# Operand tiles of 512-column matmuls moved to addresses congruent modulo 512 bytes, in a two-sequence encoder layer

## The chip, the cores and the metric

The kernel is one program on one core of a Trainium2 chip. The metric is the device time of one execution in microseconds (us); of several executions the median counts. The core's engines each work through a queue of their own: TensorE (PE in the profile; its weight loads are PEld), VectorE (DVE), ScalarE (ACT), GpSimd (POOL) and SyncE (SP, which here only starts transfers). They meet through semaphores. The on-chip memory, SBUF, has 128 partitions; "address" below is a byte offset within a partition, the same for all 128.

## The reference

One layer of an encoder, applied to two sequences (prompt and sample) of 1024 rows by 1024 columns, all in float32:

```python
h = rmsnorm(x, g_mix) * (1 + sc1) + sh1
q_lat, kv_lat, k_pe, f_in = split(h @ w_in)      # 256, 128, 64, 512 columns
y_mla  = mla_group(q_lat, kv_lat, k_pe, ...)     # 4 heads of latent attention with a rotary part
y_four = fourier_group(f_in, w_four)             # Re(FFT over rows and group columns), then 8 small products
x  = x + ga1 * (concat([y_mla, y_four]) @ w_out)
h2 = rmsnorm(x, g_ffn) * (1 + sc2) + sh2
y  = x + ga2 * ((silu(h2 @ w_gate) * (h2 @ w_up)) @ w_down)    # inner width 2816
return rmsnorm(y, g_final)
```

The six vectors sc1 to ga2 come from a small product of each sequence's conditioning vector.

## The kernel before

**Precision.** Every large float32 operand is kept as two tiles: a rounded high part (ScalarE's CAST, line 62, in `split`) and the remainder (VectorE's subtraction, line 63). A product is then three matmuls, high by high, high by low and low by high, lines 78, 79 and 80 in `mm3`. In `mm3(out, lh, ll, rh, rl, ...)` the l operands are stationary (128 columns, loaded as weights) and the r operands are moving (here mostly 512 columns, in the Fourier and attention parts also 448, 280, 258 or 256).

**Stages**, in the order of TensorE's queue and with their place in the profiled execution. Weights are folded and modulation vectors made (0 to 60 us); the input projection follows (to about 235). The Fourier part (238 to 330) multiplies by cosine and sine tables (`dft`): A holds the even-symmetric half of the frequencies, in 514 columns per 128 rows (512, and one pair of columns, 512 and 513, for frequency 512 and its filler), B the odd half in 512, `nyt` a few rows of Nyquist terms. `fourier_out` multiplies A, B and nyt, as stationary 128-column pieces, by folded weights `wm` and `wn`; the column pair goes through a product of its own for j = 0 (lines 774 to 779). Attention (332 to 769) runs 64 items (sequence s, query block b of 256 rows, head h, half u): `absorb_q` and `rope_q` make the query pieces qa and qp, `scores` multiplies them (stationary) by the latents `lat` (moving, 512 columns, 5 x 2 matmuls per item, lines 924 to 928), a softmax follows, `flip_p` transposes, `values` multiplies ckv by the probabilities, `out_proj` multiplies the result o by wv and adds it to x2. `norm2` squares (ScalarE, line 874), makes the reciprocal root (POOL, `rstd`) and scales (VectorE, line 879); the transposed result goes out to DRAM.

**The FFN** uses a seven-product scheme of the Strassen kind on 2 x 2 blocks. For each sequence the seven combinations of the input, H[0] to H[6], stand in SBUF as pairs of tiles, high H00, H10 ... H60 and low H01 ... H61, 4 x 512 columns each; `prep_h` fills them in the order HK = (0, 5, 1, 6, 4, 3, 2) by way of staging tiles H20, H21, H30, H31, X0. In the up projection (sequence 0: 778.8 to 1217.9; sequence 1: 1429.9 to 1870.1) each of 22 blocks of gate and up weights is combined into seven tiles (`sums_w`, lines 135 and 138), split into wh and wl (`hl`), and multiplied: 22 x 7 x 4 x 3 = 1848 matmuls per sequence, stationary wh or wl, moving H. In the down projection (1217.9 to 1429.9 and 1870 to 2051.5) both operands are tiles of the wh and wl rings. The last product of sequence 1 (2051.5 to 2081.6) uses H tiles on both sides, which by then hold other operands (`prep_last`).

**Memory.** Tiles are taken from pools that follow each other in the same addresses. A pool lays its tags out in the order in which the code first asks for them. Several small tiles named "phase..." hold nothing: they shift what is laid out behind them by 32 bytes. p3e is the pool of attention that `stage3_loads` lays out; p5, the pool of the FFN with all H tiles, starts at the same address when p3e is closed. A tile of p5 can be written only when the last reader of the p3e tile that it overlaps is done; the framework adds a wait for this, unless it follows from an earlier one.

**Order.** Each engine runs its queue in the order the code emits, apart from `issue_after` and `first`, which pin pieces of the transition to places behind named instructions. At the transition from attention to the FFN (lines 1014 to 1021 and 1154 to 1193) the last items of attention, `out_proj(1,2,...)`, the first H tiles (H00 and H01 from staging H20), the combinations w0 (written into H41) and `norm2` are interleaved so. `gbank` has two PSUM banks shared by `values` and `out_proj`.

Of the kernel before, what the change touches and what calls it, by code (L numbers as in the profile page):

```python
# [21 lines left out]
P = 128  # L22
# [30 lines left out]
def hybrid_encoder_kernel(ctx: ExitStack, tc: tile.TileContext, a: dict):  # L53
# [4 lines left out]
    def rd(t):  # L58
        return t.bitcast(F32)
# [104 lines left out]
    with ExitStack() as st:  # L164
# [13 lines left out]

        w.tile([P, 8], F32, name="phase_hh")
        wuqT = w.tile([P, HEADS, QL], F32, tag="hh0", name="wuqT")  # L180
        wq = w.tile([P, 2, 768], F32, tag="hl0", name="wq")
        w.tile([P, 8], F32, name="phase_wz")
        wz_h = w.tile([P, NC, DZ], F32R, name="wz_h")
# [404 lines left out]
    def load_q(s, b):  # L588
# [3 lines left out]
        S["q", s, b] = ql  # L592

    def rope_q(s, b, u, bankf):
        ql = S["q", s, b]
# [12 lines left out]
        here["p"] = nc.gpsimd.tensor_tensor(out=t1[:, 0], in0=t1[:, 0], in1=t1[:, 1], op=ALU.add).ins  # L608
        sk = e.tile([P, HEADS, P], F32R, tag="sk", name="qsk", bufs=2)
        nc.scalar.copy(sk[:, :, :64], t1[:, 0])  # L610
# [3 lines left out]
    def rope_flip(s, b, u, pt):  # L614
        sk = S.pop(("sk", s, b, u))
        for h in range(HEADS):
            nc.tensor.transpose(pt[:, h, :], sk[:, h, :], identr)
        qp = e.tile([P, HEADS, P], F32R, tag="qp", name="qp", bufs=4)
        nc.scalar.copy(qp, rd(pt))
        S["qp", s, b, u] = qp  # L620

    def absorb_q(s, b, h, bankf):
        ql = S["q", s, b]
        pq = bankf()
        hs = slice(h * P, h * P + P)
        for c in range(2):
            mm3(pq[:, :256], wq_h[:, c, hs], wq_l[:, c, hs], ql[0][:, c, :], ql[1][:, c, :], c == 0, c == 1)
        qa = [e.tile([P, 256], F32R, tag=f"qa{i}", name=f"qa{i}", bufs=3) for i in range(2)]
# [25 lines left out]
    with ExitStack() as st:  # L654
# [36 lines left out]
        def dft(s):  # L691
            z, od = zh.pop(s)
            A = [w.tile([P, 2, 528], F32R, tag=f"A{i}", name=f"A{i}", bufs=1)[:, :, :NT] for i in range(2)]
            B = [w.tile([P, 2, 512], F32R, tag=f"B{i}", name=f"B{i}", bufs=1) for i in range(2)]
            for q in (0, 2, 1) if s == 0 else (0, 1):
# [12 lines left out]
                if q == 2:  # L708
                    ah = w.tile([NY2, 528], F32R, name="nyh")[:, :NT]
                    al = w.tile([NY2, 528], F32, name="nyl")[:, :NT]  # L710
                else:
                    ah, al = A[0][:, q, :], A[1][:, q, :]
                for o, v in ((slice(0, 256), pe[:m, :256]), (slice(256, 512), po[:m, :256]), (slice(512, 514), pe[:m, 256:NTE])):
                    split(ah[:, o], al[:, o], v)
                if q == 2:
                    nc.vector.tensor_scalar(out=al, in0=al, scalar1=cmask[:m, 1:2], scalar2=None, op0=ALU.mult)
                    nc.vector.scalar_tensor_tensor(out=nyt[:m], in0=rd(ah), scalar=cmask[:m, 0:1], in1=al,
                                                   op0=ALU.mult, op1=ALU.add)
            for q in range(2):
# [34 lines left out]
        def fourier_out(s, ABn, j):  # L754
# [3 lines left out]
            for g in range(2):  # L758
# [57 lines left out]
        for s in range(2):  # L816
# [10 lines left out]
            if s == 0:  # L827
# [83 lines left out]
    with ExitStack() as st:  # L911
# [102 lines left out]
        for k in range(nit + 4):  # L1014
# [7 lines left out]
            if k < nit:  # L1022
# [5 lines left out]
                if k == nit - 1:  # L1028
                    with tc.issue_after(here["exp"]):
                        nc.scalar.activation(tiny.tile([P, 1], F32, name="warm"), cmask[:, 0:1], AF.Silu)  # L1030
                nxt = items[k + 8 - k % 8] if k + 8 - k % 8 < nit else None
# [622 lines left out]
```

## Time and profile before

| | |
|---|---|
| three executions | 2094.64, 2095.50, 2096.97 us; median 2095.5 |
| the profiled execution | 2094.11 us |
| its span, first to last instruction | 2092.3 us |
| mean granted TensorE clock | 0.991 of full |
| instructions | 28786 |

The profile is of one execution on the core. Its rows give, for groups or single instructions, the engine, the source line, the operation, the tile written and the tiles read (out<-in, numbers of buffers left out), partitions x elements and a count behind x. In groups, busy microseconds and mean nanoseconds of one follow, then the idle time of the engine just before them and what ended most of it. In a timeline a row starts with its start and its length in microseconds, and brackets hold the idle time before it with what ended it. In a table of windows, a row has the window and its length, then for PE, PEld, DVE, ACT and POOL the busy time and the number of instructions, then the granted clock, the busy share of the DMA engines and the GB/s. Matmuls overlap in the array, so the time from one start to the next (the pitch) is shorter than the length of one.

### The profile page before, as it was taken

Reading aid. Unit: us, or ns where it says so; the run is one execution under the profiler, and the core shown is the slowest. Engines: PE = TensorE matmul, PEld = TensorE weight load, DVE = VectorE, ACT = ScalarE, POOL = GpSimd, SP = SyncE. Lnnn points to the kernel's source line nnn. Section 1 sums busy time; section 2 is a strip of 40 time slices with the busy share of each in tenths; the row PEclk is TensorE's granted clock in tenths of the full one; section 3 lists DMA queues with packets and bytes.
Section 4 is the critical chain, followed back from the end, with each engine's and each line's share of the span. In section 5 each row is a group of like instructions: output and inputs, shape, how many; then the busy total and the mean of one; then the engine's idle time right before and its main releaser. Section 6 shows DMA issues by size and latency. Waiting matters only on the chain. (4 is left out here: it accounts for less than half of the span.)

```text
span 2092.3 us, 28786 instructions
## 1 busy us (share of the span) xinstructions
PE 2024.3 (97%) x10044; PEld 1665.8 (80%) x10044; DVE 1399.9 (67%) x2087; ACT 902.8 (43%) x1765; POOL 840.1 (40%) x1034
## 2 busy tenths in 40 slices
PE   5899999999999999999999999998999999999997
PEld 2788877888888877888888888886788888888876
DVE  2757757766677677767677676676765565566684
ACT  2666535555555564223323355453233333336441
POOL 1455203111313315878778510334554454420142
PEclk8999999999999999999999999999999999999999
DMA  9586774544543465546446487674332232258672
GB/s 362 196 253 196 239 259 177 132 101 101 148 110 115 167 239 179 180 173 213 167 164 216 150 281 257 216 241 143 116 126 101 76 126 101 77 176 281 222 231 91
DMA packets 182942, 371.30 MB, mean 177 GB/s; under 512 B 19020, under 2 KB 58316, under 8 KB 179724
## 3 DMA queue, kind: packets, MB, share of 16 engines
q1 hardware_dynamic: 163660, 309.80, 44.0%
q0 software_dynamic: 19136, 59.65, 9.5%
q8 instruction: 79, 1.29, 0.2%
q14 instruction: 67, 0.55, 0.1%
HBM read 257.38 MB, written 120.39 MB: 181 GB/s over the span
## 5 line engine op out<-in xcount | busy, mean ns | idle before, releaser
L78 PE MATMUL bank<-H,wh 128*128 128x512 f32 x1232 | 487.9, 396 | 11.9 <-DVE val L138 7.5
L80 PE MATMUL bank<-H,wl 128*128 128x512 f32 x1232 | 486.9, 395 | 1.9 <-DVE wl L63 1.9
L79 PE MATMUL bank<-H,wh 128*128 128x512 f32 x1232 | 487.3, 396 | 0.2 <-DVE H L63 0.2
L138 DVE TENSOR_TENSOR val<-bank,val 128x512 f32<-128x512 f32 x244 | 167.0, 689 | 199.8 <-PE bank L80 195.0
L78 PEld LDWEIGHTS bank<-H,wh 128*128 128x128 f32 x1232 | 232.7, 189 | 68.8 <-DVE val L138 9.0
L80 PEld LDWEIGHTS bank<-H,wl 128*128 128x128 f32 x1232 | 232.8, 189 | 56.5 <-DVE wl L63 2.6
L79 PEld LDWEIGHTS bank<-H,wh 128*128 128x128 f32 x1232 | 232.9, 189 | 54.3 <-DVE H L63 0.6
L63 DVE TENSOR_TENSOR wl<-draw,wh 128x512 fp32r<-128x512 f32 x286 | 200.8, 738 | 86.0 <-ACT wh L62 85.8
L62 ACT CAST wh<-draw 128x512 fp32r<-128x512 f32 x286 | 168.7, 619 | 157.8 <-PE bank L79 83.6
L138 POOL TENSOR_TENSOR val<-val 128x512 f32<-128x512 f32 x58 | 83.0, 1439 | 365.3 <-DVE val L1435 187.1
L79 PE MATMUL bank<-wl,wh 128*128 128x512 f32 x572 | 224.0, 392 | 2.0 <-DVE wl L63 2.0
L62 ACT CAST wh<-rgu 128x512 fp32r<-128x512 f32 x172 | 106.7, 621 | 271.6 <-PE bank L79 215.2
L80 PE MATMUL bank<-wh,wl 128*128 128x512 f32 x572 | 223.0, 390 | 0.0
L78 PE MATMUL bank<-wh 128*128 128x512 f32 x572 | 222.8, 390 | 0.0
L62 ACT CAST wh<-val 128x512 fp32r<-128x512 f32 x133 | 82.1, 621 | 276.6 <-PE bank L79 251.9
L63 DVE TENSOR_TENSOR wl<-val,wh 128x512 fp32r<-128x512 f32 x133 | 143.1, 1078 | 82.2 <-ACT wh L62 82.2
L135 POOL TENSOR_TENSOR val<-rgu 128x512 f32<-128x512 f32 x84 | 123.0, 1464 | 122.1 <-DMA rgu<-in_wgu_dram 118.4
L63 DVE TENSOR_TENSOR wl<-rgu,wh 128x512 fp32r<-128x512 f32 x172 | 158.2, 920 | 5.2 <-ACT wh L62 5.1
L79 PEld LDWEIGHTS bank<-wl,wh 128*128 128x128 f32 x572 | 107.4, 188 | 27.8 <-DVE wl L63 5.6
L78 PEld LDWEIGHTS bank<-wh 128*128 128x128 f32 x572 | 107.4, 188 | 22.2
L80 PEld LDWEIGHTS bank<-wh,wl 128*128 128x128 f32 x572 | 107.5, 188 | 22.0
L933 DVE TENSOR_REDUCE mx<-ps_s 128x1 f32<-128x1024 f32 x64 | 78.2, 1222 | 62.1 <-PE ps_s L928 61.5
(352 smaller groups left out, 4097.3 us busy)
## 6 DMA issues: line engine op xcount, KB each, us to landing
rgu<-in_wgu_dram SPq DMA_DIRECT2D x86, 512.0 KB
draw<-s_d SPq DMA_DIRECT2D x143, 256.0 KB
s_d<-val POOLq DMA_DIRECT2D x88, 256.0 KB, 4.1
draw<-t_d SPq DMA_DIRECT2D x88, 256.0 KB
s_d<-val SPq DMA_DIRECT2D x66, 256.0 KB
draw<-in_w_down_dram SPq DMA_DIRECT2D x55, 256.0 KB
wada<-in_w_ada_dram SPq DMA_DIRECT2D x13, 1024.0 KB
xt<-in_x_dram SPq DMA_DIRECT2D x16, 512.0 KB
```

The costliest lines, as they stand in the source:

```text
L62: here["a"] = nc.scalar.copy(hi, src).ins
L63: here["v"] = nc.vector.tensor_tensor(out=lo, in0=src, in1=rd(hi), op=ALU.subtract).ins
L78: nc.tensor.matmul(out, lh, rh, start=first, stop=False, skip_group_check=cont)
L79: nc.tensor.matmul(out, lh, rl, start=False, stop=False, skip_group_check=cont)
L80: nc.tensor.matmul(out, ll, rh, start=False, stop=last, skip_group_check=cont)
L135: return eng.tensor_tensor(out=out, in0=x, in1=y, op=ALU.subtract).ins
L138: eng.tensor_tensor(out=out, in0=x, in1=y, op=ALU.add)
L933: nc.vector.tensor_reduce(out=mx, in_=ps, axis=AX.X, op=ALU.max)
```

## The change

The arithmetic stays. Padding tiles are removed, resized or added, a few tiles are laid out in another order, and one column pair gets tiles of its own.

- The tile "phase_hh" (32 bytes) ahead of the folded query weights goes, and "phase_wz" grows from 32 to 160 bytes.
- A, nyt, nyh and nyl no longer have 528 columns. A and ny have 512; columns 512 and 513 go to tiles of their own, An and nyn; nyh and nyl get 576. The zeroing and the masking of ny, one VectorE operation each, become two each.
- In `stage3_loads` the order of first requests changes. Four small functions (`sk_tile`, `qp_tile`, `qa_tiles`, `q_tiles`) make the query tiles, so that these are laid out ahead of ql and ckv; three of four padding tiles go.
- The tile "warm", of one column, takes the tag "pc" that the tiny pool already has; all pools that follow start 128 bytes lower.

```diff
-        w.tile([P, 8], F32, name="phase_hh")
...
-        w.tile([P, 8], F32, name="phase_wz")
+        w.tile([P, 40], F32, name="phase_wz")
...
+    def sk_tile():
+        return e.tile([P, HEADS, P], F32R, tag="sk", name="qsk", bufs=2)
+
+    def qp_tile():
+        return e.tile([P, HEADS, P], F32R, tag="qp", name="qp", bufs=4)
+
+    def qa_tiles():
+        return [e.tile([P, 256], F32R, tag=f"qa{i}", name=f"qa{i}", bufs=3) for i in range(2)]
+
+    def q_tiles():
+        sk_tile()
+        qa_tiles()
+        qp_tile()
...
     def stage3_loads():
         wq_h = e.tile([P, 2, 768], F32R, name="wq_h")
         wq_l = e.tile([P, 2, 768], F32R, name="wq_l")
-        e.tile([P, 8], F32, name="phase_ql")
-        load_q(0, 0)
-        e.tile([P, 8], F32, name="phase_hv")
-        hv = [half("hv") for _ in range(2)]
+        half("hv")
         rc = e.tile([P, 8, ROPE], F32, name="rc")
         rs = e.tile([P, 8, ROPE], F32, name="rs")
         lat = [e.tile([P, 2, N], F32R, tag=f"lat0{i}", name=f"lat0{i}") for i in range(2)]
-        e.tile([P, 8], F32, name="phase_kv")
+        q_tiles()
+        e.tile([P, 8], F32, name="phase")
+        load_q(0, 0)
         for c in range(2):
...
-        e.tile([P, 8], F32, name="phase_e")
...
-        nyt = w.tile([P, 528], F32R, name="ny")[:, :NT]
-        nc.vector.tensor_scalar(out=nyt, in0=raws[0, 0], scalar1=0.0, scalar2=None, op0=ALU.mult)
+        An = [w.tile([P, 2, 2], F32R, name=f"An{i}") for i in range(2)]
+        nyn = w.tile([P, 2], F32R, name="nyn")
+        nyt = w.tile([P, 512], F32R, name="ny")
+        for t, sl in ((nyt, slice(0, 512)), (nyn, slice(512, 514))):
+            nc.vector.tensor_scalar(out=t, in0=raws[0, 0][:, sl], scalar1=0.0, scalar2=None, op0=ALU.mult)
...
-            A = [w.tile([P, 2, 528], F32R, tag=f"A{i}", name=f"A{i}", bufs=1)[:, :, :NT] for i in range(2)]
+            A = [w.tile([P, 2, 512], F32R, tag=f"A{i}", name=f"A{i}", bufs=1) for i in range(2)]
...
-                        mm3(pn[:2, :], A[0][:, q, 512:514], A[1][:, q, 512:514], wm[0][:, q, gs], wm[1][:, q, gs], q == 0, False)
-                    nc.tensor.matmul(pn[:2, :], ny[:, 512:514], wn[:, gs], start=False, stop=True)
+                        mm3(pn[:2, :], An[0][:, q, :], An[1][:, q, :], wm[0][:, q, gs], wm[1][:, q, gs], q == 0, False)
+                    nc.tensor.matmul(pn[:2, :], nyn, wn[:, gs], start=False, stop=True)
...
-                    nc.scalar.activation(tiny.tile([P, 1], F32, name="warm"), cmask[:, 0:1], AF.Exp)
+                    nc.scalar.activation(tiny.tile([P, 1], F32, tag="pc", name="warm"), cmask[:, 0:1], AF.Exp)
```

Start addresses of the tiles in the two built programs, modulo 512 bytes:

| tiles (use) | before | after |
|---|---|---|
| H00 to H61 (up projection moving; last product) | 96 | 480 |
| wh, wl, val, wv, o, pt, lat10, lat11 | 480 | 480 |
| lat00, lat01 (scores, sequence 0, moving) | 160 | 480 |
| qa, qp (scores, stationary), qsk | 224 | 480 |
| wq | 96 | 480 |
| ql | 128 | 0 |
| ckv | 192 | 0 |
| A0 and A1 | 352 and 480, second rows 64 further | 224 |
| B / ny | 96 / 288 | 224 / 224 |
| wm, wn | 224 | 224 |
| wz (projection, moving, 448 columns) | 160 or 416 | 128 or 384 |
| hh, hl (projection, stationary) | 128 or 256 | 480 or 224 |

The attention tiles that lie under four H tiles also change:

| H tile | before | after |
|---|---|---|
| H31 | lat01, ckv0 | qa0, qa1, qp |
| H41 | ckv0 (its last 96 bytes), ckv1, qsk | qp, ql0 |
| H00 | qsk, qa0, qa1, qp | ql0, ql1, ckv0 |
| H01 | qp, the gate row (gah) | ckv0, ckv1, gah |

The order of instructions stays the same on all engines but for a few neighbours. What changes at the transition from attention to the FFN is waits. On ScalarE's queue there, before (o0b13 is the high part of an attention output, written from a bank gb of `values`; xn is the square for `norm2`):

```order
L62 CAST o0b13_8282<-gb_8492 128x256 [waits PE_49]
L62 CAST H00_8632<-H20_8612 128x1024 [waits DMAHW3_49,Activation_49]
L62 CAST H00_8632<-H20_8612 128x1024 [waits DMAHW4_49]
L874 ACTIVATE xn_8535,ms2_8534<-x2_8311 128x1024 [waits DMAHW1_49,DVE_49]
L62 CAST o0b13_8282<-gb_8562 128x256 [waits PE_49]
L62 CAST H50_8645<-H21_8622 128x1024 [waits DMAHW0_49]
```

And now:

```order
L62 CAST o0b13_8286<-gb_8496 128x256 [waits PE_49]
L62 CAST H00_8636<-H20_8616 128x1024 [waits DMAHW3_49,PE_49]
L62 CAST H00_8636<-H20_8616 128x1024 [waits DMAHW4_49]
L891 ACTIVATE xn_8539,ms2_8538<-x2_8315 128x1024 [waits DMAHW1_49,DVE_49]
L62 CAST o0b13_8286<-gb_8566 128x256 [waits PE_49]
L62 CAST H50_8649<-H21_8626 128x1024 [waits DMAHW0_49]
```

No row moved (line 874 has become 891). The first cast into H00 now waits for TensorE, and the count it waits for is reached by a matmul of line 79 in the last `values`, one before the last of all; that product's bank is gb_8566, whose reader stands three rows further down.

On VectorE's queue at the same place, before (gb_8519 and gb_8548 are two banks of `out_proj(1,2,...)`, H41 and rgu0 the combinations w0):

```order
L866 TENSOR_TENSOR x2_8311<-x2_8311,gb_8519 128x512 [waits PE_49]
L63 TENSOR_TENSOR H01_8633<-H20_8612,H00_8632 128x1024 [waits DMAHW3_49,Activation_49]
L63 TENSOR_TENSOR H01_8633<-H20_8612,H00_8632 128x1024 [waits DMAHW4_49,Activation_49]
L866 TENSOR_TENSOR x2_8361<-x2_8361,gb_8548 128x512 [waits DMAHW7_49,DMAHW2_49,PE_49]
L879 TENSOR_SCALAR xn_8535<-x2_8311,rs_r_8540 128x1024 [waits Activation_49,Pool_49]
L63 TENSOR_TENSOR o1b13_8283<-gb_8562,o0b13_8282 128x256 [waits Activation_49]
L135 TENSOR_TENSOR H41_8631<-rgu0_8615 128x512 [waits DMAHW6_49,PE_49]
```

And now:

```order
L883 TENSOR_TENSOR x2_8315<-x2_8315,gb_8523 128x512 [waits PE_49]
L63 TENSOR_TENSOR H01_8637<-H20_8616,H00_8636 128x1024 [waits DMAHW3_49,DMAHW4_49,PE_49,Activation_49]
L63 TENSOR_TENSOR H01_8637<-H20_8616,H00_8636 128x1024 [waits DMAHW4_49,Activation_49]
L883 TENSOR_TENSOR x2_8365<-x2_8365,gb_8552 128x512 [waits DMAHW7_49,DMAHW2_49]
L896 TENSOR_SCALAR xn_8539<-x2_8315,rs_r_8544 128x1024 [waits Activation_49,Pool_49]
L63 TENSOR_TENSOR o1b13_8287<-gb_8566,o0b13_8286 128x256 [waits Activation_49]
L135 TENSOR_TENSOR H41_8635<-rgu0_8619 128x512 [waits DMAHW6_49]
```

Again no row moved (866 and 879 have become 883 and 896). The first operation into H01 now waits for the last matmul of `values`; the one into H41 no longer waits for it; and the addition of the second bank needs no wait of its own for TensorE any more, since the one two rows ahead of it is later.

More of the change, by code (lines that the diff above doesn't have):

```diff
@@ L608, in rope_q @@
         here["p"] = nc.gpsimd.tensor_tensor(out=t1[:, 0], in0=t1[:, 0], in1=t1[:, 1], op=ALU.add).ins
-        sk = e.tile([P, HEADS, P], F32R, tag="sk", name="qsk", bufs=2)
+        sk = sk_tile()
         nc.scalar.copy(sk[:, :, :64], t1[:, 0])
@@ L617, in rope_flip @@
             nc.tensor.transpose(pt[:, h, :], sk[:, h, :], identr)
-        qp = e.tile([P, HEADS, P], F32R, tag="qp", name="qp", bufs=4)
+        qp = qp_tile()
         nc.scalar.copy(qp, rd(pt))
@@ L627, in absorb_q @@
             mm3(pq[:, :256], wq_h[:, c, hs], wq_l[:, c, hs], ql[0][:, c, :], ql[1][:, c, :], c == 0, c == 1)
-        qa = [e.tile([P, 256], F32R, tag=f"qa{i}", name=f"qa{i}", bufs=3) for i in range(2)]
+        qa = qa_tiles()
         split(qa[0], qa[1], pq[:, :256])
@@ L708, in dft @@
                 if q == 2:
-                    ah = w.tile([NY2, 528], F32R, name="nyh")[:, :NT]
-                    al = w.tile([NY2, 528], F32, name="nyl")[:, :NT]
-                else:
-                    ah, al = A[0][:, q, :], A[1][:, q, :]
-                for o, v in ((slice(0, 256), pe[:m, :256]), (slice(256, 512), po[:m, :256]), (slice(512, 514), pe[:m, 256:NTE])):
-                    split(ah[:, o], al[:, o], v)
+                    ah = w.tile([NY2, 576], F32R, name="nyh")
+                    al = w.tile([NY2, 576], F32, name="nyl")
+                    parts = [(ah[:, o : o + n], al[:, o : o + n]) for o, n in ((0, 256), (256, 256), (512, 2))]
+                else:
+                    parts = [(A[0][:, q, o : o + 256], A[1][:, q, o : o + 256]) for o in (0, 256)]
+                    parts.append((An[0][:, q, :], An[1][:, q, :]))
+                for (vh, vl), v in zip(parts, (pe[:m, :256], po[:m, :256], pe[:m, 256:NTE])):
+                    split(vh, vl, v)
                 if q == 2:
-                    nc.vector.tensor_scalar(out=al, in0=al, scalar1=cmask[:m, 1:2], scalar2=None, op0=ALU.mult)
-                    nc.vector.scalar_tensor_tensor(out=nyt[:m], in0=rd(ah), scalar=cmask[:m, 0:1], in1=al,
-                                                   op0=ALU.mult, op1=ALU.add)
+                    nc.vector.tensor_scalar(out=al[:, :NT], in0=al[:, :NT], scalar1=cmask[:m, 1:2], scalar2=None, op0=ALU.mult)
+                    for t, o in ((nyt, slice(0, 512)), (nyn, slice(512, 514))):
+                        nc.vector.scalar_tensor_tensor(out=t[:m], in0=rd(ah[:, o]), scalar=cmask[:m, 0:1], in1=al[:, o],
+                                                       op0=ALU.mult, op1=ALU.add)
             for q in range(2):
@@ L1029, in hybrid_encoder_kernel @@
                     with tc.issue_after(here["exp"]):
-                        nc.scalar.activation(tiny.tile([P, 1], F32, name="warm"), cmask[:, 0:1], AF.Silu)
+                        nc.scalar.activation(tiny.tile([P, 1], F32, tag="pc", name="warm"), cmask[:, 0:1], AF.Silu)
                 nxt = items[k + 8 - k % 8] if k + 8 - k % 8 < nit else None
```

## The prediction

> **What bounds the kernel now.** I read the page's busy line first, then the largest groups, then windows of the long stages, then the timeline at the one place where the change adds a wait.
>
> ```profile
> span 2092.3 us, 28786 instructions
> PE 2024.3 (97%) x10044; PEld 1665.8 (80%) x10044; DVE 1399.9 (67%) x2087; ACT 902.8 (43%) x1765; POOL 840.1 (40%) x1034
> L78 PE MATMUL bank<-H,wh 128*128 128x512 f32 x1232 | 487.9, 396 | 11.9 <-DVE val L138 7.5
> ```
>
> TensorE is busy for 97% of the span, and the group that costs most, one of three alike in the up projection (L78 to L80, 3 x 1232 = 3696 matmuls), waits 11.9 us in all. So the span is mostly a count of matmuls times their pitch (start to start; the 396 ns of the row is longer, since matmuls overlap). The windows give the pitch by stage; the number behind x counts the matmuls, one or two at the edges included.
>
> ```profile
> 850.00:1200.00 350.00, 350.00 (x1507) 284.12 (x1507) 248.65 (x253) 107.20 (x180) 271.73 (x249) 1.00 0.53 181
> 1240.00:1360.00 120.00, 120.00 (x531) 99.41 (x530) 84.94 (x126) 63.66 (x117) 20.31 (x16) 1.00 0.74 249
> 1500.00:1860.00 360.00, 360.00 (x1551) 292.25 (x1550) 210.02 (x259) 110.18 (x185) 167.36 (x140) 1.00 0.29 102
> 1880.00:2010.00 130.00, 130.00 (x573) 107.38 (x573) 90.97 (x134) 68.40 (x124) 17.93 (x15) 1.00 0.74 247
> 2053.00:2080.00 27.00, 27.00 (x121) 22.38 (x120) 15.70 (x27) 3.70 (x11) 12.74 (x41) 1.00 0.32 117
> ```
>
> All five have TensorE busy throughout at full granted clock (1.00) and nothing but 128x512 products. With 1.5 taken off each count for the edges, the up projection (first and third row) runs at 232.5 and 232.3 ns, the down projection (second and fourth) at 226.6 and 227.5, the last products, H tiles on both sides, at 226. By the built program's addresses the stationary tiles of the up projection start at 480 modulo 512 and its moving tiles at 96; in the down projection both start at 480, in the last products both at 96. The slow stage is the one where they differ. H tiles alone are not at fault, since they run at 226 against each other; nor is the other engines' load, since the third row has less DMA than the second and a slower pitch.
>
> Attention repeats this within one kind of matmul, the scores (L924 to L928), for the two sequences, whose latents stand at different addresses:
>
> ```profile
> 491.57 0.40 PE L925 MATMUL ps_s<-lat,qa 128*128 128x512 f32 x1
> ...
> 493.44 0.40 PE L928 MATMUL ps_s<-lat,qp 128*128 128x512 f32 x1
> ...
> 683.43 0.39 PE L924 MATMUL ps_s<-lat,qa 128*128 128x512 f32 x1
> ...
> 685.47 0.39 PE L928 MATMUL ps_s<-lat,qp 128*128 128x512 f32 x1
> ```
>
> Sequence 0 (160 against 224, 64 apart): 8 steps in 1.87 us, 234 ns. Sequence 1 (480 against 224, 256 apart): 9 steps in 2.04 us, 227 ns. So a distance of 256 seems as good as none, and 64 and 128 (which is 96 against 480) cost 5 to 7 ns.
>
> **The change part by part.** *Up projection.* H moves from 96 to 480, so all 3696 matmuls become like those of the down projection. The rows allow 232.4 - 227.0 = 5.4 ns each (4.8 to 6.4 by the single rows). Not all of it is paid out, because two stretches are paced by VectorE:
>
> ```profile
> 778.00:815.00 37.00, 31.74 (x141) 24.68 (x139) 34.93 (x39) 21.25 (x36) 18.17 (x19) 1.00 0.50 176
> L78 PE MATMUL bank<-H,wh 128*128 128x512 f32 x71 | 29.2, 411 | 7.2 <-DVE val L138 3.8 <-ACT val L1334 3.1 <-ACT wh L62 0.4
> ```
>
> The first is the start for sequence 0 (VectorE busy 34.9 of 37 us), which I stretch to 833 (190 matmuls); the second is the window 1430 to 1490, 3 x 71 = 213 matmuls with 7.2 us of waits. A faster matmul there waits longer for VectorE. That leaves 3293 x 5.4 = 17.8 us (15 with the low end; 20 if those stretches pay too).
>
> *Scores.* Sequence 0 becomes congruent, 320 matmuls. A run of ten is cut off by transposes, so I take 4 of the 7 ns: 1.3 us (0 to 2.2). Sequence 1 goes from 256 apart to 0: nothing.
>
> *Smaller places.* About 236 products of the Fourier output with A, B and ny, and about 190 of the input projection, move off bad distances. By the same rows 0 to 7 ns each, 0 to 3 us; I take 1.7. The 256-column products were and stay off; nothing. Two more VectorE operations of 128x2 and 48x2 stand off the path behind splits of the same stage; nothing, and well under 1 us if that cover went. The warm tile's new tag adds no wait.
>
> *The new wait.* Renumbering the attention pool moves ckv0 and ckv1 from under H31 and H41 to under H00 and H01, the tiles that are filled first. The last readers of ckv are the last products with the values. These are the rows of ACT, VectorE and TensorE around it:
>
> ```profile
> 753.11 0.37 ACT L62 CAST o0b<-gb 128x256 fp32r<-128x256 f32 x1 [1.59 <-PE gb L80]
> 753.38 2.00 ACT L62 CAST H<-H 128x1024 fp32r<-128x1024 f32 x2
> 756.59 1.06 ACT L874 ACTIVATE xn<-x 128x1024 f32<-128x1024 f32 x1 [1.21 <-DVE x L866]
> 757.56 0.19 ACT L874 ACTIVATION_READ_ACCUMULATOR xn<-x 128x1 f32 x1
> 761.40 0.37 ACT L62 CAST o0b<-gb 128x256 fp32r<-128x256 f32 x1 [3.65 <-PE gb L80]
> ```
> ```profile
> 756.48 2.35 DVE L63 TENSOR_TENSOR H<-H,H 128x1024 fp32r<-128x1024 f32 x2
> 758.75 0.68 DVE L866 TENSOR_TENSOR x<-x,gb 128x512 f32<-128x512 f32 x1
> 760.69 0.76 DVE L879 TENSOR_SCALAR xn<-x,rs_r 128x1024 f32<-128x1024 f32 x1 [1.26 <-POOL rs_r L110]
> 761.80 0.42 DVE L63 TENSOR_TENSOR o1b<-gb,o0b 128x256 fp32r<-128x256 f32 x1 [0.36 <-ACT o0b L62]
> 762.15 0.68 DVE L135 TENSOR_TENSOR H<-rgu 128x512 f32<-128x512 f32 x1
> ...
> 764.92 0.68 DVE L866 TENSOR_TENSOR x<-x,gb 128x512 f32<-128x512 f32 x1
> ...
> 769.74 0.76 DVE L879 TENSOR_SCALAR xn<-x,rs_r 128x1024 f32<-128x1024 f32 x1 [1.27 <-POOL rs_r L110]
> ```
> ```profile
> 761.20 0.40 PE L78 MATMUL gb<-wv,o0b 128*128 128x512 f32 x1
> ...
> 769.39 0.27 PE L1146 MATMUL pht<-ident,xn 128*128 128x128 f32 x1
> 770.55 0.99 PE L1146 MATMUL pht<-ident,xn 128*128 128x128 f32 x7 [0.89 <-DVE xn L879]
> ```
>
> In the clock of before: the two casts of H00 (753.38) now wait for the value products, whose end released o0b at 761.40; they run 761.3 to 763.3. Behind them in ACT's queue the square of L874 runs 763.3 to 764.5. VectorE's two H01 operations follow the casts, 762.4 to 764.7, and hold the L866 behind them, which empties the second gb bank: 764.7 to 765.4 instead of 758.75. TensorE needs that bank for the matmul at 761.20 and stands still 4.2 us. The L879 waits for the square and, as before, 2.9 us of POOL (757.75 to 760.69): 767.5. Then o1b at 768.1, four L135 from 768.5 (2.77 us, as 762.15 to 764.92), the next L866 at 771.2 instead of 764.92, and the next L879 at 776.0 instead of 769.74, since between the two only ACT, POOL and VectorE work at their old durations. TensorE's transposes at 770.55 wait for it: 776.9. From there until about 794 TensorE waits on this same VectorE chain, so I see nothing that absorbs the delay: 6.3 us lost (0 if VectorE had slack I overlook; 7.9 if the whole shift of the casts, 753.4 to 761.3, came through). The load of H31, which waited for the same value products, comes free earlier; no one waits for it, so nothing.
>
> One more price hangs on the standstill.
>
> ```profile
> 1483.81 0.40 PE L80 MATMUL bank<-H,wl 128*128 128x512 f32 x1
> 1486.36 0.76 PE L78 MATMUL bank<-H,wh 128*128 128x512 f32 x1 [2.16 <-DVE val L138]
> ...
> 1489.89 0.39 PE L80 MATMUL bank<-H,wl 128*128 128x512 f32 x1
> ```
>
> After 2.16 us of idleness eight matmuls took 3.53 us where 1.86 is usual, a loss of 1.7. After the new 4.2 us this may come too, but then TensorE's next 24 matmuls (5.5 us, or 7.2) end before VectorE's 776.0, so I take 0 and keep 1.7 as the upper end. The Trainium skill (TensorE: Matmul & The Clock Gate, Why this matters for your kernels) says that idle gaps over about 3 us send the clock to half; here one of 2.16 us did.
>
> *Sum.* The profiled execution took 2094.1 us, 1.8 more than its span. 2094.1 - 17.8 - 1.3 - 1.7 + 6.3 = 2079.6. The median of the runs shown, 2095.5, is 1.4 above that execution: **2081 us**.
>
> **The rivals.** *The wait is absorbed:* the pitch gains as above and the 6.3 us vanish: 2074.7. For it, VectorE idles 1.3 us twice in these rows; against it, those pauses are ends of the very ACT and POOL chain that is shifted.
>
> *Half the gain:* the pitch falls only part of the way, or another engine takes over. POOL is busy 271.7 of 350 us and VectorE 248.7 in the first row of the windows; 2.3% less time leaves both short of full, which speaks against it. For it: matmuls that resume after a wait may need a while to fall into the fast pitch, as the cut-up scores suggest. With 10.4 instead of 20.8: 2091.4.
>
> *The pitch has nothing to do with addresses* and the up projection is slow for what it is. Then only the wait is left: 2095.5 + 6.3 = 2101.8, slower. It decides as soon as the gain is under 0.6 ns per up-projection matmul (2.1 us in all against 6.3). Against it stand the scores, one kind at two pitches, and H at 226. The Trainium skill has a rule for this outcome: the same page (Part 2: What happens when you issue a matmul) states that TensorE has two independent read ports, so loading the next weights takes nothing from a running matmul. By that rule alone addresses could not matter; the windows disagree, 232 against 227 ns.
>
> **How the numbers follow.** Forecast 65%, wait absorbed 15%, half the gain 13%, no gain 7%. The forecast's own bounds are 2076 to 2087 (pitch terms 2 to 5 us either way, the wait 1.6, the clock 1.7). For 8 in 10 I reach to the absorbed wait below and to half the gain above: 2073 to 2091. A measurement of this kernel tells about 0.2%, 4.2 us, from no change. Faster by more (under 2091.3): the forecast, the absorbed wait and about half of the half gain, 0.87. Within: the rest of that and a little of no gain, 0.07. Slower: 0.06.
>
> **What would show it.** The windows of the up projection should have 1 matmul per 227 ns, with 3 x 1232 still there; the scores of sequence 0 should step by 227 to 230. On ACT the first H00 cast should start right after the last value product, with TensorE idle about 4 us before the next product with wv, and the first up-projection matmul some 6 us later, counted from that last value product. Wrong it would be by a pitch above 229 in the windows, by a cast that does not wait, or by a new stall elsewhere, above all at the start of the second up projection, where VectorE already sets the pace.

## The result and the profile after

| | median, us | runs, us |
|---|---|---|
| before | 2096.2 | 2094.64 to 2097.48 (4) |
| changed | 2079.9 | 2078.84 to 2083.78 (4) |

The ratio is 0.9926 (95% interval 0.9909 to 0.9943): 0.7% faster, 16 us by the medians. Predicted were 2081 us and a range of 2073 to 2091.

The first lines of the changed kernel's page, and the first of the three up-projection groups:

```profile
span 2078.6 us, 28790 instructions
PE 2008.3 (97%) x10044; PEld 1667.0 (80%) x10044; DVE 1413.0 (68%) x2089; ACT 903.1 (43%) x1765; POOL 837.3 (40%) x1034
L78 PE MATMUL bank<-H,wh 128*128 128x512 f32 x1232 | 482.2, 392 | 9.7 <-DVE val L138 5.0
```

The count of matmuls is the old one, 10044 in all and 1232 in the group. TensorE's share is still 97%: it was busy before and is busy now, and only the pitch can have changed. It stands in the windows (for each, the length, then PE's busy time and number of instructions):

```profile
850.00:1200.00 350.00, 350.00 (x1545) 289.79 (x1544) 271.65 (x259) 110.08 (x185) 277.21 (x253) 1.00 0.56 185
1240.00:1360.00 120.00, 119.53 (x527) 98.44 (x526) 82.24 (x124) 62.44 (x113) 19.59 (x16) 1.00 0.73 245
1500.00:1860.00 360.00, 360.00 (x1590) 298.09 (x1589) 213.24 (x265) 113.84 (x191) 167.39 (x144) 1.00 0.30 106
```

With 1.5 taken off for the edges as before, the up projection now runs at 226.8 and 226.6 ns (1545 matmuls in the same 350 us that held 1507). The granted clock was 1.00 then and is 1.00 now. VectorE runs 259 instructions in the first window where it ran 253, and POOL 253 where it ran 249, since the work that belongs to a matmul comes faster. VectorE's busy time rose by 9%, more than its count; why is open. Neither reaches its limit.

Now the transition from attention to the FFN, in the timelines of ScalarE, VectorE and TensorE (start, length, then the group; in brackets the idle time before it and what ended it):

```profile
753.23 0.37 ACT L62 CAST o0b<-gb 128x256 fp32r<-128x256 f32 x1 [1.61 <-PE gb L80]
761.42 1.99 ACT L62 CAST H<-H 128x1024 fp32r<-128x1024 f32 x2 [7.82 <-PE gb L79]
763.32 1.05 ACT L891 ACTIVATE xn<-x 128x1024 f32<-128x1024 f32 x1
```
```profile
762.50 2.36 DVE L63 TENSOR_TENSOR H<-H,H 128x1024 fp32r<-128x1024 f32 x2 [5.84 <-ACT H L62]
764.78 0.68 DVE L883 TENSOR_TENSOR x<-x,gb 128x512 f32<-128x512 f32 x1
766.73 0.75 DVE L896 TENSOR_SCALAR xn<-x,rs_r 128x1024 f32<-128x1024 f32 x1 [1.27 <-POOL rs_r L110]
...
770.51 0.68 DVE L883 TENSOR_TENSOR x<-x,gb 128x512 f32<-128x512 f32 x1
...
775.33 0.75 DVE L896 TENSOR_SCALAR xn<-x,rs_r 128x1024 f32<-128x1024 f32 x1 [1.27 <-POOL rs_r L110]
```
```profile
761.22 0.28 PE L80 MATMUL gb<-pt,ckv 128*128 128x256 f32 x1
765.51 0.58 PE L78 MATMUL gb<-wv,o0b 128*128 128x512 f32 x1 [4.01 <-DVE x L883]
765.89 0.63 PE L79 MATMUL gb<-wv,o0b 128*128 128x512 f32 x1
...
769.26 0.40 PE L78 MATMUL gb<-wv,o0b 128*128 128x512 f32 x1
...
784.43 0.39 PE L78 MATMUL bank<-H,wh 128*128 128x512 f32 x1
```

ScalarE stands idle for 7.82 us in front of the H00 casts, released by a matmul of line 79 of the last value product. VectorE's H01 operations follow, the addition that empties the second bank comes at 764.78 instead of 758.75, and TensorE idles 4.01 us, named for just that addition. The first up-projection matmul starts at 784.43; it was 778.84.

Cut at the first matmul of each stage, the two profiled executions compare so:

| stage | before, us | after, us | difference |
|---|---|---|---|
| start to the last value product | 761.08 | 761.22 | +0.1 |
| from there to the first up-projection matmul | 17.76 | 23.21 | +5.5 |
| up projection, sequence 0 | 439.07 | 429.64 | -9.4 |
| down projection, sequence 0 | 212.03 | 213.03 | +1.0 |
| up projection, sequence 1 | 440.12 | 429.68 | -10.4 |
| the rest | 222.2 | 221.8 | -0.4 |
| span | 2092.3 | 2078.6 | -13.7 |

In the down projection, 1.0 us longer, two splits came late near 1358 us, with TensorE waiting 0.23 us for each and slower for three matmuls around them. The eleven kernels below took 211.9 to 215.2 us for this stage, so 1.0 us is within what differs from one execution to the next.

### The profile page after: what moved, and what is told of

It reads as the page before. It is cut to its first block, busy times and chain, and to the rows that moved or that the text cites. A ratio compares the mean times of both kernels' runs of the same rounds, so it can differ in the third digit from the quotient of the medians.

```text
span 2078.6 us, 28790 instructions
## 1 busy us (share of the span) xinstructions
PE 2008.3 (97%) x10044; PEld 1667.0 (80%) x10044; DVE 1413.0 (68%) x2089; ACT 903.1 (43%) x1765; POOL 837.3 (40%) x1034
## 5 line engine op out<-in xcount | busy, mean ns | idle before, releaser
L78 PE MATMUL bank<-H,wh 128*128 128x512 f32 x1232 | 482.2, 392 | 9.7 <-DVE val L138 5.0
L80 PE MATMUL bank<-H,wl 128*128 128x512 f32 x1232 | 481.4, 391 | 1.4 <-DVE wl L63 1.4
L79 PE MATMUL bank<-H,wh 128*128 128x512 f32 x1232 | 481.9, 391 | 0.4 <-DVE H L63 0.4
L78 PEld LDWEIGHTS bank<-H,wh 128*128 128x128 f32 x1232 | 232.7, 189 | 60.6 <-DVE val L138 6.1
L80 PEld LDWEIGHTS bank<-H,wl 128*128 128x128 f32 x1232 | 232.7, 189 | 50.5 <-DVE wl L63 1.9
L79 PEld LDWEIGHTS bank<-H,wh 128*128 128x128 f32 x1232 | 232.6, 189 | 49.0 <-DVE H L63 0.8
L79 PE MATMUL bank<-wl,wh 128*128 128x512 f32 x572 | 223.9, 391 | 1.9 <-DVE wl L63 1.9
L78 PE MATMUL bank<-wh 128*128 128x512 f32 x572 | 222.7, 389 | 0.2 <-ACT wh L62 0.2
L80 PE MATMUL bank<-wh,wl 128*128 128x512 f32 x572 | 222.7, 389 | 0.0
L63 DVE TENSOR_TENSOR wl<-rgu,wh 128x512 fp32r<-128x512 f32 x172 | 165.8, 964 | 4.3 <-ACT wh L62 4.3
L79 PEld LDWEIGHTS bank<-wl,wh 128*128 128x128 f32 x572 | 107.3, 188 | 27.8 <-DVE wl L63 5.7
L78 PEld LDWEIGHTS bank<-wh 128*128 128x128 f32 x572 | 107.4, 188 | 23.1 <-ACT wh L62 0.7
L80 PEld LDWEIGHTS bank<-wh,wl 128*128 128x128 f32 x572 | 107.4, 188 | 22.0
```

Source lines behind the costliest of these rows:

```text
L63: here["v"] = nc.vector.tensor_tensor(out=lo, in0=src, in1=rd(hi), op=ALU.subtract).ins
L78: nc.tensor.matmul(out, lh, rh, start=first, stop=False, skip_group_check=cont)
L79: nc.tensor.matmul(out, lh, rl, start=False, stop=False, skip_group_check=cont)
L80: nc.tensor.matmul(out, ll, rh, start=False, stop=last, skip_group_check=cont)
```

## The experiments

Eleven kernels ran. Two theories were to be told apart from their rivals: that the whole gain is the up projection's pitch, and that this is set by the distance between the addresses of the moving and the stationary tiles; and that the new wait costs what the transition shows.

**The wait taken away from the changed kernel.** ckv0 and ckv1 go under H31 (and the first bytes of H41), and the query tiles behind them:

```diff
-        q_tiles()
-        e.tile([P, 8], F32, name="phase")
-        load_q(0, 0)
+        sk_tile()
+        e.tile([P, 8], F32, name="phase")
+        for c in range(2):
+            e.tile([P, 8, KVL], F32R, tag=f"ckv{c}", name=f"ckv{c}", bufs=1)
+        load_q(0, 0)
+        e.tile([P, 120], F32, name="phase_qa")
+        qa_tiles()
+        qp_tile()
```

> The changed kernel with ckv0 and ckv1 laid under H31 and H41 instead of H00 and H01; ql, qa and qp move along, and all 512-column operands keep their addresses modulo 512. The first H00 cast then no longer waits for the last value product. Theory (the new wait is on the path that sets the end): the first up-projection matmul starts some 5.6 us earlier than in the changed kernel, and the time falls from 2079.9 to about 2074 (2072.5 to 2076). Rival (VectorE has slack before the up projection that takes the wait up anyway, and the later start has another cause): 2079 to 2081, the first up-projection matmul within 1 us of the changed kernel's.

Measured: 2074.97 us against 2094.0 of before on the same chip, ratio 0.9909 (0.9896 to 0.9923). ScalarE's and TensorE's timelines there:

```profile
751.81 2.00 ACT L62 CAST H<-H 128x1024 fp32r<-128x1024 f32 x2
755.03 1.06 ACT L896 ACTIVATE xn<-x 128x1024 f32<-128x1024 f32 x1 [1.22 <-DVE x L888]
```
```profile
759.67 0.40 PE L78 MATMUL gb<-wv,o0b 128*128 128x512 f32 x1
...
777.30 0.39 PE L78 MATMUL bank<-H,wh 128*128 128x512 f32 x1
```

The casts start without an idle time, the wv product follows the values at once, and the up projection starts 7.1 us earlier than in the changed kernel. 5.5 of these lie in the transition; the other 1.7 were there before it. That is spread: six profiled executions with these addresses reached the last value product at 758.8 to 762.7 us. The theory holds, the rival is out.

**The H tiles alone moved.** To the kernel before, one line:

```diff
         w = st.enter_context(tc.tile_pool(name="p5", bufs=1, reuse_waits="tile"))
+        w.tile([P, 96], F32, name="phase")
```

> The kernel before with one padding tile of 384 bytes ahead of all tiles of the FFN pool, so that the H tiles start at 480 modulo 512, and nothing else changed. Theory (the gain of the change is the up projection's pitch, set by the distance of H from wh and wl): 226.7 ns instead of 232.4 per up-projection matmul, 2096.2 - 3696 x 5.4 to 5.7 ns = 2075 to 2077, and no gain elsewhere. Rival (the gain needs the other tiles too, latents and Fourier tiles among them, as the prediction's terms of 1.3 and 1.7 us said): about 2079 or above, since 3 us would be missing.

Measured: 2074.9 us, ratio 0.9909 (0.9894 to 0.9925), the same as the kernel above, in which latents, wq, A, B and ny have the new addresses too. The windows of the two up projections:

```profile
850.00:1200.00 350.00, 350.00 (x1545) 289.81 (x1544) 260.61 (x258) 109.68 (x184) 272.41 (x249) 1.00 0.55 185
1500.00:1840.00 340.00, 340.00 (x1502) 281.53 (x1501) 200.70 (x251) 106.66 (x179) 159.46 (x136) 1.00 0.30 105
```

226.8 and 226.6 ns. So 384 bytes of padding bring all of the gain, and none of the loss. The other moved tiles bring nothing that can be measured in the total, to within the 3 us or so of these intervals; the rival, which is two terms of the prediction, falls. The stages before the FFN are compared further down.

**The wait alone.** The kernel before with the attention pool in the new order, and padding that keeps the old distances:

```diff
-        e.tile([P, 8], F32, name="phase_ql")
-        load_q(0, 0)
-        e.tile([P, 8], F32, name="phase_hv")
+        e.tile([P, 16], F32, name="phase_hv")
...
-        e.tile([P, 8], F32, name="phase_kv")
+        e.tile([P, 16], F32, name="phase_q")
+        e.tile([P, HEADS, P], F32R, tag="sk", name="qsk", bufs=2)
+        for i in range(2):
+            e.tile([P, 256], F32R, tag=f"qa{i}", name=f"qa{i}", bufs=3)
+        e.tile([P, HEADS, P], F32R, tag="qp", name="qp", bufs=4)
+        e.tile([P, 40], F32, name="phase_ql")
+        load_q(0, 0)
+        e.tile([P, 16], F32, name="phase_kv")
...
-        e.tile([P, 8], F32, name="phase_e")
```

> The kernel before with its attention pool laid out in the order of the changed kernel (query tiles, then ql, then ckv under H00 and H01), with padding that keeps H, latents, query tiles and wq at their old addresses modulo 512. Theory: the new wait alone costs 5.6 to 6.3 us, 2096.2 + 6 = 2102 (2101 to 2104), with TensorE idle some 4 us after the last value product. Rival (absorbed): 2096 to 2097.

Measured: 2099.8 us against 2094.0, ratio 1.0034 (1.0021 to 1.0048): slower by 5.8 us. The timelines repeat the changed kernel's, idle time for idle time:

```profile
760.38 1.99 ACT L62 CAST H<-H 128x1024 fp32r<-128x1024 f32 x2 [7.82 <-PE gb L79]
```
```profile
764.47 0.79 PE L78 MATMUL gb<-wv,o0b 128*128 128x512 f32 x1 [4.01 <-DVE x L870]
...
783.80 0.40 PE L78 MATMUL bank<-H,wh 128*128 128x512 f32 x1
```

2099.8 is below the expected 2101 to 2104, which were counted from a before of 2096.2; here before took 2094.0. The difference of 5.8 is inside what the theory foresaw (5.6 to 6.3).

**Which distance.** Three runs ask what about the addresses counts. In the first the H tiles stay and the pool of wh, wl and val moves to 96 (the kernel before; 384 bytes of padding at that pool's end):

```diff
-            return w5.tile([P, 512], F32, tag="v", name="val", bufs=VALS)
+            v = w5.tile([P, 512], F32, tag="v", name="val", bufs=VALS)
+            if "end" not in S:
+                S["end"] = w5.tile([P, 96], F32, name="phase_end")
+            return v
```

> The kernel before with H left at 96 modulo 512 and the pool of wh, wl and val moved down by 384 bytes instead, so that these start at 96 too (a padding tile at the pool's end). Theory (only the distance counts): up projection at 226.7 ns and the same time as with H moved, ratio 0.991 (2074 to 2077). Rival (480 is a good address in itself, or 96 a bad one): up projection stays at 232, or the down projection gets slower, ratio 0.997 to 1.01.

In the second the one-line padding of the H-only kernel is 128 bytes (`w.tile([P, 32], ...)`):

> The kernel before with 128 bytes of padding ahead of the FFN pool: H at 224, 256 from wh and wl. Theory (the distance counts modulo 256): 226.7 ns, ratio 0.991. Rival (it counts modulo 512, as the change's words say): 232 ns, ratio 1.00.

Measured: 2075.6 us, ratio 0.9907 (0.9892 to 0.9922), and 2075.7 us, ratio 0.9906 (0.9890 to 0.9921), against 2095.3 of before. The windows, the ring at 96 first, H at 224 second:

```profile
850.00:1200.00 350.00, 350.00 (x1545) 289.67 (x1545) 267.35 (x258) 109.56 (x184) 273.42 (x249) 1.00 0.56 185
```
```profile
850.00:1200.00 350.00, 350.00 (x1545) 289.67 (x1544) 269.09 (x258) 110.14 (x185) 274.52 (x249) 1.00 0.56 185
```

Two other pairs of addresses, 96 with 96 and 224 with 480, give the same 1545 matmuls as 480 with 480. So neither 480 nor 96 is good or bad in itself; the distance is what counts, and 256 is as good as 0.

The changed kernel ran once more beside these:

> The changed kernel again, beside the others on one chip. Theory (the single padding tile brings the whole gain, the other moved addresses nothing that can be measured, and the new wait costs 5.5 us): slower than the kernels with the distance alone put right by 5 to 6 us, ratio 0.9935 to 0.994. Rival (the other moves bring 2 to 3 us): ratio 0.992 or less.

Measured: 2082.0 us, ratio 0.9938 (0.9921 to 0.9954), 6.3 and 6.4 us over the two kernels above, a little more than the expected 5 to 6. The theory holds: the changed kernel is the gain of the padding less the wait.

**Other distances.** First seven at once, by padding between the H tiles of the changed kernel:

```diff
+        DIST = {"2": 0, "3": 32, "41": 32, "0": 64, "5": 96, "1": 128, "40": 160, "6": 192}
+        cur = [0]
+        seen = set()
+
         def quad(tag, dt=F32):
+            if tag[0] == "H" and tag not in seen:
+                seen.add(tag)
+                n = (DIST.get(tag[1:], DIST.get(tag[1])) - cur[0]) % 512
+                cur[0] += n
+                if n:
+                    w.tile([P, n // 4], F32, name="phase" + tag)
```

> The changed kernel with padding between the H tiles, so that in one run the up projection's seven products have their moving tiles at different distances from the stationary ones, modulo 256: H2 0, H3 32, H0 64, H5 96, H1 128, H6 192, and H40 160 with H41 32. Theory 1 (any distance other than 0 modulo 256 is slow, as the latents at 64 and the old H at 128 were): H2 at 227 ns, all others at 231 to 234. Theory 2 (the cost grows with the distance up to 128 and falls again): 32 and 192 between 227 and 232. Theory 3 (the address of the moving tile itself counts, not the distance): no such pattern; H1, which stands at the old 96, would still be slow. By theory 1 the total is near 2098.

Measured in one execution: 2100.6 us. Mean steps of the products: 230.3 ns at 64, 234.0 at 96, 233.2 at 128, 231.4 at 160 with 32, 233.5 at 32, 232.5 at 192. The product at distance 0, H2, has 229.7, and it is worth reading matmul by matmul. It is the last of the seven and follows the H3 product, at 32:

```profile
1618.57 0.40 PE L80 MATMUL bank<-H,wl 128*128 128x512 f32 x1
1618.81 0.40 PE L78 MATMUL bank<-H,wh 128*128 128x512 f32 x1
1619.05 0.39 PE L79 MATMUL bank<-H,wh 128*128 128x512 f32 x1
...
1620.43 0.39 PE L79 MATMUL bank<-H,wh 128*128 128x512 f32 x1
1620.66 0.39 PE L80 MATMUL bank<-H,wl 128*128 128x512 f32 x1
...
1621.56 0.40 PE L78 MATMUL bank<-H,wh 128*128 128x512 f32 x1
```

The first row is the last matmul of H3, the second the first of H2, the last the next product. From 1618.81 to 1620.66 the eight steps take 1.85 us, 231 ns each; the last four, to 1621.56, take 0.90 us. Over all 44 products the mean of step i is 240.6, 224.4, 230.8, 235.7, 228.4, 232.3, 230.8, 226.7, 226.6, 226.7, 226.7, 226.6. So a congruent product that follows one at a bad distance gets its pitch only after some seven matmuls here. The means of the other distances are spoilt in the same way, each product being twelve long.

Therefore two runs with all H tiles at one distance, 192 and 352 bytes of padding in the H-only kernel:

> The kernel before with 192 bytes of padding ahead of the FFN pool: H at 288, 192 below wh and wl, which is 64 modulo 256. All 3696 matmuls then have the distance that the latents of sequence 0 had. Theory (any distance but 0 modulo 256 costs 5 to 7 ns): 231 to 234 ns in the up projection, a total of 2090 to 2098. Rival (only some distances are slow, and the run with several distances was spoilt by its changes from product to product): 227 to 229 ns, about 2076 to 2083.

> The kernel before with 352 bytes of padding: H at 448, only 32 below wh and wl. Theory (any distance but 0 modulo 256): 231 to 234 ns, 2090 to 2098 in all. Rival (tiles 32 bytes apart are as good as congruent): 227 ns, about 2075.

Measured: 2084.3 and 2098.0 us, beside 2094.9 of before, one execution each. The windows, H at 288 first, at 448 second:

```profile
850.00:1200.00 350.00, 349.88 (x1529) 286.76 (x1528) 265.11 (x256) 108.16 (x182) 272.67 (x249) 1.00 0.56 184
```
```profile
850.00:1200.00 350.00, 350.00 (x1501) 281.77 (x1500) 247.18 (x251) 106.75 (x180) 271.31 (x249) 1.00 0.53 180
```

229.1 and 233.4 ns. With H 32 bytes below the weights the theory holds, and the up projections are a little slower than before. With H at 288 the theory falls: the cost is 2.3 ns over the best pitch, not 5 to 7, which is the upper end of the rival (227 to 229).

The distance has a direction, which the expectations overlook. Counted from the stationary tile up to the moving one, modulo 256, H at 288 is at 64, H at 448 at 224 (not 32), and H of before at 128. The latents of sequence 0, at 160 against 224, are 64 below, which is 192. So the run at 288 did not have their distance, as its expectation says, and does not contradict their 233 ns. In the kernel with several distances the product at 192 (H6) alternates between steps of some 235.7 and 231.0 ns once it has settled, while the one at 64 (H0) settles at a mean of 228.9. The last eight steps of such an H6 product take 1.87 us:

```profile
1611.36 0.40 PE L79 MATMUL bank<-H,wh 128*128 128x512 f32 x1
...
1613.23 0.39 PE L78 MATMUL bank<-H,wh 128*128 128x512 f32 x1
```

So the distance is no yes-or-no matter, nor does the cost grow with it, and 64 above is not 64 below: 0 and 256 give 226.7 ns, 64 gives 229, 128 (before) 232.4, 192 and 224 give 233 to 234.

**Which of the two weights.** While a matmul streams, the weights of the next are loaded. The rows of TensorE and of its weight loads in the first of the two next kernels show it:

```profile
1600.35 0.40 PE L79 MATMUL bank<-H,wh 128*128 128x512 f32 x1
1600.58 0.40 PE L80 MATMUL bank<-H,wl 128*128 128x512 f32 x1
1600.82 0.39 PE L78 MATMUL bank<-H,wh 128*128 128x512 f32 x1
```
```profile
1600.35 0.19 PEld L80 LDWEIGHTS bank<-H,wl 128*128 128x128 f32 x1
```

The load of wl for line 80 starts with the matmul of line 79. Two kernels were to show whether the distance to the weights in use or to those being loaded counts. In the one the ring of wl is 128 bytes off:

```diff
                 w5.tile([P, 2, 512], F32, tag="ga", name="tdb", bufs=1)
+                w5.tile([P, 32], F32, name="phase_wl")
+                w5.tile([P, 512], F32R, tag="wl", name="wl", bufs=8)
+                w5.tile([P, 96], F32, name="phase_v")
```

> The changed kernel with the ring of wl tiles 128 bytes further (96 modulo 512) and wh and H left at 480. In the up projection only line 80 (wl by the high H) then has a distance of 128 between its own two operands; while line 79 runs, the weights of line 80 are loaded. Theory 'next' (a moving tile is slowed by the weights loaded beside it): the step from line 79's start to line 80's is the slow one, 230 to 237 ns. Theory 'own' (by the weights in use): the step from line 80's start. Theory 3 (the steps are locked together, so that one bad distance in three spoils them all): all three lines at 229 to 233. In each case the up projection loses at least a third of its gain, 2085 to 2102 in all.

In the other the low parts of H are:

```diff
+        for t in ("H20", "X0", "X1", "H30", "H40", "H00", "H50", "H10", "H60"):
+            quad(t)
+        w.tile([P, 32], F32, name="phase_low")
+        for t in ("H21", "H31", "H41", "H01", "H51", "H11", "H61"):
+            quad(t)
         H = {}
```

> The changed kernel with the H tiles in another order in memory: high parts at 480 modulo 512 as before, low parts at 96, so that only line 79 has a distance (128) from the weights in use and from the weights loaded beside it (wl, 480). This takes up what the run with wl moved left open: there the steps from line 79 and from line 80 were both slow (232.5 and 234.1 ns), the step from line 78 not (226.8). Theory A (both pairs count: the moving tile with the weights in use and with those being loaded): only the step from line 79 is slow here, lines 78 and 80 at 227. Theory B (a bad step spoils the next one too): lines 79 and 80 slow, 232 and 234, line 78 at 227, as with wl moved. The H tiles come to lie over other attention tiles, so the transition to the FFN may differ; the total is not the point.

Measured, one execution each: 2098.4 and 2090.1 us (before: 2095.3 and 2094.9), and as mean steps in ns in the up projection (850 to 1200 us for sequence 0, 1500 to 1840 for sequence 1):

| | from L78 | from L79 | from L80 |
|---|---|---|---|
| H, wh, wl congruent (changed kernel) | 226.8 | 226.6 | 226.8 |
| wl off by 128 | 226.8 | 232.5 | 234.1 |
| low H off by 128, sequence 0 | 231.0 | 229.6 | 233.2 |
| low H off by 128, sequence 1 | 226.7 | 234.1 | 225.9 |

No theory fits all of this. With wl off, line 79's step is slow, which has the bad distance only to the weights being loaded, and so is line 80's, which has it only to the weights in use. Theory A was drawn from this. With the low H off it holds in sequence 1, where only the step from line 79 is slow. In sequence 0, with the same tiles at the same addresses, it fails: that step is the fastest of the three, and the steps repeat every six matmuls (means of 232.5, 231.6, 234.2, 229.2, 227.5 and 231.7 ns) instead of every three. The windows of the two sequences:

```profile
850.00:1200.00 350.00, 350.00 (x1515) 284.08 (x1514) 256.51 (x254) 107.31 (x180) 277.26 (x251) 1.00 0.54 182
1500.00:1840.00 340.00, 340.00 (x1487) 278.43 (x1486) 197.62 (x247) 105.06 (x177) 166.69 (x140) 1.00 0.30 105
```

231.2 and 228.9 ns: off the congruent distance, the same addresses can run in two steady patterns with different pitches. What puts a sequence into one or the other (its first matmuls, or the load of the other engines, which differs), and what couples one step to the next, remains open.

## Why the prediction was right, step by step

*The place of the bound.* Right: TensorE's count times pitch, with the granted clock at 1.00, and the count did not change.

*The up projection.* Right in its mechanism, a little small. It gave 17.8 us, 3293 matmuls by 5.4 ns; measured are 19.9. The pitch fell by 5.7 ns, as far as the down projection's. The start of sequence 0 gained nothing, as foreseen: its first 216 instructions on TensorE took 56.1 us in both kernels. But the second stretch put down as paced by VectorE, 1430 to 1490, did pay: its first 228 matmuls took 63.7 us before and 62.5 after, with one wait of 1.6 us gone and another 0.6 us longer.

*The new wait.* Right, with the chain as drawn: casts at 761.42 (predicted 761.3), the bank emptied from 764.78 (764.7), TensorE idle 4.0 us (4.2), the second scaling at 775.33 (776.0). The delay was 5.5 instead of 6.3 us, because the first scaling, behind POOL's six small operations, came at 766.73 and not at 767.5: the first of the six took 0.39 us, and 1.08 before. The wait-only kernel prices it at 5.8 us by itself. The rival "absorbed" is out.

*The clock after the standstill.* Nine matmuls from 765.51 to 769.26 took 3.75 us where nine at 227 ns take 2.04. The granted clock there is 0.54. These 1.7 us were foreseen as possible and as free, and they were: TensorE still idles 0.43 us for VectorE's second scaling, until 776.14. An idle time does not always have this price: in the kernel before, 2.16 us (to 1486.36) were followed by a clock of 0.52, but 3.06 us (to 1440.20) by one of 1.00.

*Scores and the smaller places.* Right in the pitch, wrong in the time, by 3.0 us: 1.3 and 1.7 us were expected, and the changed kernel reached the last value product 0.1 us later than before. It is not chance of one execution: the seven profiled executions with the old distances before the FFN reached it at 760.7 us on average (760.2 to 761.3), the six with the new ones at 760.8 (758.8 to 762.7). Yet the scores of sequence 0 did speed up, from a median step of 233 ns to 227, and from 2365 to 2324 ns for an uninterrupted run of ten. Here is the run that the prediction read, now eight steps in 1.83 us instead of 1.87:

```profile
490.73 0.39 PE L942 MATMUL ps_s<-lat,qa 128*128 128x512 f32 x1
...
492.56 0.40 PE L945 MATMUL ps_s<-lat,qp 128*128 128x512 f32 x1
```

That is some 1.1 us over the sequence, and the Fourier products with A, B and ny are another 0.7 us shorter. The step that failed is that such a gain is paid out. TensorE also waits for VectorE's part of the softmax there, and these waits grew; between 332 and 536 us they are, in the kernel before and in the changed one:

```profile
PE ppt L950 <- DVE nb L934: 1.5, 1, 1.5
PE ppt L950 <- DVE p L938: 0.3, 2, 0.2
```
```profile
PE ppt L967 <- DVE nb L951: 1.9, 2, 1.6
PE ppt L967 <- DVE p L955: 0.7, 4, 0.2
```

On average over the same executions, TensorE's waits in attention grew by 1.0 us, and attention as a whole did not get shorter (429.5 and 429.7 us). Part of the rest are the value products, put at nothing: ckv moved too, from 32 to 224 against pt, and they took some 0.6 us more. The input projection shows nothing beyond its spread.

*The rival "addresses do not matter"* is out: four kernels in which nothing but the start of the H tiles differs have 226.8, 226.8, 229.1 and 233.4 ns. The Trainium skill (TensorE: Matmul & The Clock Gate, Part 2: What happens when you issue a matmul) has a matmul and the next weight load read through two independent ports; these runs do not agree with independence, whatever couples the two: with only wl off, the step from line 79, whose own two tiles are congruent, took 232.5 ns instead of 226.6. *Half the gain* is out for the whole, but its reason, that a pitch must settle, shows in the short runs: ten scores gained 41 ns and not ten times 6.

The sum came out near the measurement, -14.5 against -13.7 us of the profiled execution, since the missing 3.0 was made up by 2.1 more in the up projection and 0.8 less for the wait. That these errors cancel is luck; the 1.0 of the down projection is spread.

## What to carry to other kernels

Where one product of long, uninterrupted matmuls runs a few per cent slower than another of the same shape at the same clock, compare the start addresses of its moving and stationary tiles, modulo 256; padding ahead of the pool of one of them may be all that is needed. A faster pitch saves time where TensorE waits for nothing else, as in the up projection; in attention it went mostly into longer waits. Moving tiles in memory also moves what lies under them later: after any change of layout, look for new waits of the next stage's first writers on the last readers of this one. Here that took back about a quarter of the gain, and the version with one padding tile, or with ckv laid under H31, takes 2075 us and beats both kernels.

## What the runs showed of the hardware that was not expected

A matmul of 128x512 in steady flow took 226.7 ns with its moving tile 0 or 256 bytes from its stationary tile. Counted upwards from the stationary tile, modulo 256, it took 229 ns at 64, 232.4 at 128 and 233 to 234 at 192 and 224: neither in order of the distance nor all alike, and not the same in the two directions. A product that became congruent after another that was not needed about seven matmuls to reach its pitch. And with one bad distance among three matmuls, the same addresses ran in two steady patterns, at 231 ns in one sequence and 229 in the other.
